# One 512-column product of the high weight part for both parts of a split activation

## The chip, the cores and the metric

The kernel runs on one core of a Trainium2 chip. The metric is the device time of one execution in microseconds, lower being better. Three runs of the kernel before gave 1787.77, 1788.87 and 1789.88 us. A core has a matrix engine (TensorE, PE in the profile; its weight loads are shown apart as PEld), a vector engine (DVE), a scalar engine (ACT), a general engine (POOL) and a queue engine (SP) that here issues most transfers from HBM.

## The reference

One layer on 256 tokens of width 2048: a normalised input, one large projection, four small branches (a gated recurrence, attention, a state-space branch, an RWKV branch), a gated merge, an output projection, a feed-forward part with a short convolution, and a per-layer embedding. Cut to its large products:

```python
xn = rmsnorm(h, mix_norm[i])
proj = jnp.einsum('bsd,dn->bsn', xn, w_in[i])
...
merged = merged + gates[:, :, j] * jnp.einsum('bsc,cd->bsd', branches[j], w_branch[i, j])
h = h + jnp.einsum('bsd,de->bse', merged, w_out[i])
hn = rmsnorm(h, ffn_norm[i])
u = causal_dwconv(jnp.einsum('bsd,df->bsf', hn, w_up[i]), ffn_conv_w[i], ffn_conv_b[i])
u_gate, u_val = jnp.split(u, 2, axis=-1)
h = h + jnp.einsum('bsf,fd->bsd', jax.nn.gelu(u_gate) * u_val, w_down[i])
pg = jax.nn.sigmoid(jnp.einsum('bsd,de->bse', rmsnorm(h, ple_norm[i]), w_ple_gate[i]))
h = h + pg * jnp.einsum('bsq,qd->bsd', p[i], w_ple[i])
```

All arrays are 32-bit floats.

## The kernel before

Every large product runs in a reduced 32-bit format (`fp32r`), with each operand written as a high part plus a low part. A weight w is wh + wl, an activation x is xh + xl, and the product is taken as wh·xh + wh·xl + wl·xh. Activations lie feature-major: 128 features on the partitions, 256 tokens along the free axis.

`gemm_fm` (L222) computes a unit of 256 output features, as two halves `m` of 128. It walks over the k blocks of 128 input features in chunks of four: one transfer of 128x1024 weights (`chunk`, L194, four buffers `wr`), then `split` (L199), which makes `wh` on ACT (L206) and `wl` on DVE (L207) in pieces of 128x512, six buffers each. For each m and each k, PE then does three products of 256 columns into the same PSUM tile: wh with xh, wh with xl, wl with xh. I call these three a triple. At the unit's end `evac` reads the PSUM tile, mostly with one DVE operation that also multiplies by the token's norm R.

The order of the stages: the projection `w_ax` (L43 of the start, with x loaded and split beside it by `load_x`), 19 units of the projection `w_p`, the 2-unit token-major `w_v` (`gemm_tm`, L265: its products stream 512 weight columns over stationary activations), then four rounds of gate units (`w_g`, 16 k blocks) and branch products (`w_branch`, 4 k blocks), then `w_out` (8 units), `w_up` (44 units), `w_down` (8 units of 44 k blocks), and `w_ple`/`w_ple_gate` (8 units). The small products of the four branches (`psB` banks, L135) are put between the large ones by `pump`, one step per m and chunk.

A scheduler orders the instructions of each engine from priorities: loads, splits and evacuations are in lane "g" and go first, the branches ("b") follow, the stream of products ("m") comes last except on PE. Each engine then runs its own list in order.

The names in the rows: `s`, `sb` and `f` are 128x256 activation tiles, `pg` and `pb` PSUM banks of 512 columns, `prm` and `prm2` parameter columns, L132 the stream's matmul and L135 the branches', L100 and L120 the DVE helpers `tt` and `stt`, L127 the ACT helper.

Of the kernel before, what the change touches and what calls it, by code (L numbers as in the profile page):

```python
# [14 lines left out]
P = 128  # L15
S = 256
# [11 lines left out]
# column offsets of the input projection  # L28
# [4 lines left out]
# rows of the parameter blocks that are turned into per-partition columns  # L33
# [52 lines left out]
def body(tc, T, out, dbg=None):  # L86
# [59 lines left out]
    # The stream of products goes first on every engine but the tensor engine,  # L146
    # where the branches' small products go first.
# [11 lines left out]
    sp = ctx.enter_context(tc.tile_pool(name="sp", bufs=57))  # L159
# [20 lines left out]
    def dslot():  # L180
        return dp.tile([P, 512], F32, name="d", tag="d")
# [9 lines left out]
    # --------------------------------------------------------------- products  # L191
# [19 lines left out]
    def split_act(src, scale=None, pool=sp):  # L211
        """hi/lo parts of an activation tile (scale: per-partition column or number)."""
        h, l = slot(F32R, pool), slot(F32R, pool)
        if scale is None:
            A.copy(h, src)
            tt(l, src, h.bitcast(F32), ALU.subtract)
        else:
            act(h, src, AF.Copy if isinstance(scale, float) else AF.Identity, scale=scale)
            stt(l, src, scale, h.bitcast(F32), ALU.mult, ALU.subtract)
        return h, l  # L220

    def gemm_fm(W, xs, evac, each=None):  # L222
# [4 lines left out]
        pts = [(gbank if m < 2 else bank)()[:, :S] for m in range(nm)]  # L227
        step = 1024 // ncol
        k0 = 0
        if each is not None:  # L230
            lane("m")
            for i in range(5):
                mm(pts[0], warm[:, :P], warm, start=i == 0, stop=False)
        while k0 < nk:
# [11 lines left out]
            for m in range(nm):  # L246
                ms = slice(m * P, m * P + P)
                for k in range(kn):
                    xh, xl = xs[k0 + k]
                    wh, wl = w[k]  # L250
                    first, last = k0 + k == 0 and not (each and m == 0), k0 + k == nk - 1
                    mm(pts[m], wh[:, ms], xh, start=first, stop=False)
                    mm(pts[m], wh[:, ms], xl, start=False, stop=False)
                    mm(pts[m], wl[:, ms], xh, start=False, stop=last)
# [10 lines left out]
    def gemm_tm(W, xs, evac):  # L265
        """out[token, 512 columns] = x W, x feature-major; W: [chunk, p, k * n]."""
        nk = len(xs)
        pts = [gbank() for _ in range(2)]
        for k0 in range(0, nk, 2):
# [3 lines left out]
            for t in range(2):  # L273
                tsl = slice(t * P, t * P + P)
                for k in range(2):
                    xh, xl = xs[k0 + k]
# [12 lines left out]
    def mm2(o, l, src, start=True, stop=True, pool=sp):  # L289
        """l^T src for an l that float32r holds exactly"""  # L290
# [993 lines left out]
```

## Time and profile before

| | |
|---|---|
| median of three runs | 1788.87 us |
| span of the profiled execution, first to last instruction | 1792.8 us |
| PE busy / weight loads busy | 1784.0 us / 1763.7 us |
| DVE busy / ACT busy | 1236.4 us / 987.8 us |
| matmul records | 14953 |
| HBM read | 324.85 MB |

The profiled execution is a run of its own; its span stands 3.9 us (0.2%) above the median of the runs. Busy shares of PE overlap (a matmul's record is longer than the step from one start to the next), so what PE needs per product is read from the starts in the timeline, not from the mean duration.

### The profile page before, as it was taken

To read this page: it belongs to the slowest core of one execution; us is meant where nothing else is said; L and a number is where in the kernel's file an instruction comes from. 1 tells how busy PE (TensorE), PEld (TensorE's weight loads), DVE (VectorE), ACT (ScalarE), POOL (GpSimd) and SP (SyncE) were. 2 spreads that over 40 slices of the span, in tenths; PEclk is the share of its full clock that TensorE was granted. 3 is DMA by queue.
4 is the path that set the end of the run, shared out by engine and by line. 5 is a ranking of instruction groups with operands and counts; after the bars stand their busy time and mean duration, and the time that the engine had idled before them with its cause. 6 is when DMAs were issued, how large, how long until landed. Compare 5 with 4: busy or idle time off the path is not lost.

```text
span 1792.8 us, 37987 instructions
## 1 busy us (share of the span) xinstructions
PE 1784.0 (100%) x14953; PEld 1763.7 (98%) x14953; DVE 1236.4 (69%) x2382; ACT 987.8 (55%) x1809; POOL 102.1 (6%) x160
## 2 busy tenths in 40 slices
PE   9999999999999999999999999999999999999998
PEld 8999899999999999999999999999999999999998
DVE  8778677687789533758677777777777755555665
ACT  7677455567744433645556555555555544444543
POOL 3000000012310100000110000000000100000000
PEclk9999999999999989999999999999999999999999
DMA  8566556567775733566766666565666766665564
GB/s 277 171 182 187 172 174 218 169 190 200 210 198 171 238 117 114 178 199 189 242 212 183 182 188 182 183 185 180 184 183 186 219 194 183 189 185 180 176 211 130
DMA packets 98883, 336.80 MB, mean 188 GB/s; under 512 B 12330, under 2 KB 16592, under 8 KB 98704
## 3 DMA queue, kind: packets, MB, share of 16 engines
q1 hardware_dynamic: 90528, 310.94, 57.0%
q0 software_dynamic: 7456, 21.81, 4.0%
q8 instruction: 117, 1.92, 0.4%
q10 hardware_dynamic: 720, 1.63, 0.2%
q14 instruction: 62, 0.51, 0.1%
HBM read 324.85 MB, written 9.48 MB: 186 GB/s over the span
## 4 chain that ended last, share of the span: by engine, by line
PE 97%; DMA 1%; DVE 1%; ACT 0%; issue 0%; POOL 0%; DVEq 0%
PE pg L132 92%; PE pb L135 5%; PE pb L132 1%; DMA wr<-in_w_ax_dram 1%; DMA e<-ssd_ac 0%; DVE wl L207 0%; ACT wh L206 0%; DVE s L120 0%; DMA ssd_ac<-sb 0%; ACT s L127 0%; DVE e L116 0%; DVE s L100 0%; POOL d L432 0%; DVE sb L114 0%; DVE sb L100 0%
## 5 line engine op out<-in xcount | busy, mean ns | idle before, releaser
L132 PE MATMUL pg<-s,wh 128*128 128x256 f32 (+1 forms) x6944 | 1269.8, 284 | 2.7 <-ACT s L127 1.9
L132 PEld LDWEIGHTS pg<-s,wh 128*128 128x128 f32 (+1 forms) x6944 | 1086.1, 192 | 7.0 <-ACT s L127 2.1
L207 DVE TENSOR_TENSOR wl<-wr,wh 128x512 fp32r<-128x512 f32 x1170 | 798.2, 690 | 401.4 <-ACT wh L206 326.5
L206 ACT CAST wh<-wr 128x512 fp32r<-128x512 f32 x1170 | 712.3, 618 | 575.9 <-PE pg L132 416.8
L132 PE MATMUL pg<-s,wl 128*128 128x256 f32 (+1 forms) x3472 | 985.0, 284 | 0.4 <-DVE wl L207 0.4
L132 PEld LDWEIGHTS pg<-s,wl 128*128 128x128 f32 (+1 forms) x3472 | 664.6, 192 | 2.7 <-issue 1.0
L132 PE MATMUL pg<-f,wh 128*128 128x256 f32 x1408 | 253.5, 283 | 0.0
L132 PEld LDWEIGHTS pg<-f,wh 128*128 128x128 f32 x1408 | 219.6, 192 | 0.0
L132 PE MATMUL pg<-f,wl 128*128 128x256 f32 x704 | 199.2, 283 | 0.0
L132 PE MATMUL pg<-sb,wh 128*128 128x256 f32 x768 | 141.0, 283 | 0.0
L132 PEld LDWEIGHTS pg<-f,wl 128*128 128x128 f32 x704 | 135.2, 192 | 0.0
L120 DVE SCALAR_TENSOR_TENSOR s<-s,prm 128x255 f32<-128x255 f32 (+1 forms) x208 | 99.7, 480 | 37.5 <-ACT s L127 37.5
L132 PEld LDWEIGHTS pg<-sb,wh 128*128 128x128 f32 x768 | 119.4, 190 | 0.4
L127 ACT ACTIVATE s<-s,prm 128x256 f32<-128x256 f32 (+1 forms) x120 | 69.0, 575 | 80.4 <-DVE s L100 80.4
L132 PE MATMUL pg<-sb,wl 128*128 128x256 f32 x384 | 108.3, 283 | 0.0
L127 ACT ACTIVATE s<-s 128x256 f32<-128x256 f32 x140 | 57.7, 414 | 59.2 <-DVE s L100 39.8
L100 DVE TENSOR_TENSOR s<-pg,R 128x256 f32<-128x256 f32 x152 | 63.6, 421 | 31.8 <-PE pg L132 30.9
L132 PEld LDWEIGHTS pg<-sb,wl 128*128 128x128 f32 x384 | 72.7, 190 | 0.3 <-issue 0.2
L127 ACT ACT_TABLE_LOAD x42 | 53.9, 1283 | 2.2 <-PEq L1274 1.2
L100 DVE TENSOR_TENSOR s<-s 128x256 f32<-128x256 f32 x126 | 52.5, 419 | 0.4
L100 DVE TENSOR_TENSOR sb<-sb 128x256 fp32r<-128x256 f32 (+4 forms) x78 | 32.0, 418 | 8.6 <-ACT sb L127 6.8
L127 ACT ACTIVATE sb<-sb 128x256 f32<-128x256 f32 (+4 forms) x69 | 27.8, 414 | 9.3 <-DVE sb L100 8.1
(208 smaller groups left out, 842.6 us busy)
## 6 DMA issues: line engine op xcount, KB each, us to landing
wr<-in_w_up_dram SPq DMA_DIRECT2D x176, 512.0 KB, 3.7
wr<-in_w_g_dram SPq DMA_DIRECT2D x128, 512.0 KB, 4.0
wr<-in_w_down_dram SPq DMA_DIRECT2D x88, 512.0 KB, 3.8
wr<-in_w_p_dram SPq DMA_DIRECT2D x76, 512.0 KB, 3.9
wr<-in_w_branch_dram SPq DMA_DIRECT2D x32, 512.0 KB, 4.3
wr<-in_w_out_dram SPq DMA_DIRECT2D x32, 512.0 KB, 4.2
wr<-in_w_ple_gate_dram SPq DMA_DIRECT2D x32, 512.0 KB, 4.3
wr<-in_w_v_dram SPq DMA_DIRECT2D x8, 512.0 KB, 4.3
```

The lines of the kernel that those rows point to most:

```text
L100: V.tensor_tensor(o, a, b, op=op)
L120: V.scalar_tensor_tensor(o, a, s, b, op0=op0, op1=op1)
L127: A.activation(o, i, f, **kw)
L132: return f(*a, **kw)
L135: f(*a, **kw)
L206: A.copy(wh, wr[:, k:k + n])
L207: V.tensor_tensor(wl, wr[:, k:k + n], wh.bitcast(F32), op=ALU.subtract)
```

## The change

The two parts of an activation now lie side by side in one tile x of 512 columns. A new function `product` replaces the triple by two matmuls: wh with all 512 columns, into both halves of the 512-column bank, and wl with the first 256 columns, into the first half. From the second k block on, wl goes before wh. The two halves of the bank are added when the unit is evacuated: `joined` copies the second half out on ACT and adds the first half on DVE. Gates, branch products, the small logits and `w_v` keep three products of 256 (or 512) columns, on slices of the same tiles (`halves`). `split` makes one ACT and one DVE instruction for a whole chunk of up to 1024 columns, with three buffers each in place of six of 512.

```diff
     def split(wr, kn, cols):
-        res, step = [], max(1, 512 // cols)
-        for k in range(0, kn, step):
-            n = min(step, kn - k)
-            wh = wp.tile([P, n, cols], F32R, name="wh", tag="wh", bufs=6)
-            wl = wp.tile([P, n, cols], F32R, name="wl", tag="wl", bufs=6)
-            A.copy(wh, wr[:, k:k + n])
-            V.tensor_tensor(wl, wr[:, k:k + n], wh.bitcast(F32), op=ALU.subtract)
-            res += [(wh[:, i], wl[:, i]) for i in range(n)]
-        return res
+        wh = wp.tile([P, kn, cols], F32R, name="wh", tag="wh", bufs=3)
+        wl = wp.tile([P, kn, cols], F32R, name="wl", tag="wl", bufs=3)
+        A.copy(wh, wr)
+        V.tensor_tensor(wl, wr, wh.bitcast(F32), op=ALU.subtract)
+        return [(wh[:, i], wl[:, i]) for i in range(kn)]
...
+    def split_x(src, scale=None, to=None):
+        t = xslot() if to is None else to
+        split_to(t[:, :S], t[:, S:], src, scale)
+        return t
...
+    def product(pt, xs, k, nk, ms, w, fresh=True):
+        wh, wl = w
+        x = xs[k]
+        if k == 0:
+            mm(pt, wh[:, ms], x, start=fresh, stop=False)
+            mm(pt[:, :S], wl[:, ms], x[:, :S], start=False, stop=False)
+        else:
+            mm(pt[:, :S], wl[:, ms], x[:, :S], start=False, stop=False)
+            mm(pt, wh[:, ms], x, start=False, stop=k == nk - 1)
...
+    def joined(o, pt):
+        A.copy(o, pt[:, S:])
+        add(o, o, pt[:, :S])
...
             lane("m")
-            for i in range(5):
+            for i in range(3):
                 mm(pts[0], warm[:, :P], warm, start=i == 0, stop=False)
...
+                    if not isinstance(xs[k0 + k], tuple):
+                        product(pts[m], xs, k0 + k, nk, ms, w[k], not (each and m == 0))
+                        continue
...
-    warm = slot()
+    warm = bc_.tile([P, 512], F32, name="e", tag="e", bufs=3)
...
             s = bslot()
-            tt(s, pt, R, ALU.mult)
+            joined(s, pt)
+            mul(s, s, R)
...
+    xg = [halves(x) for x in xs]
...
-        gemm_fm(T["w_g"][8 * j + u], xs, ev_g)
+        gemm_fm(T["w_g"][8 * j + u], xg, ev_g)
...
             h = slot()
-            add(h, pt, r)
-            xs_out.append(split_act(h, norm(k)))
+            joined(h, pt)
+            add(h, h, r)
+            xs_out.append(split_x(h, norm(k)))
...
             a, o = slot(), slot()
-            tt(a, pt, R2, ALU.mult)
+            joined(a, pt)
+            mul(a, a, R2)
...
-            o = slot()
-            mul(o, pt, R3)
+            o, e = slot(), slot()
+            joined(o, pt)
+            mul(o, o, R3)
             act(o, o, AF.Sigmoid)
-            mul(o, o, pe_[m])
+            joined(e, pe_[m])
+            mul(o, o, e)
```

On PE, in the middle of `w_up`, the list of before goes through the k blocks of one half m like this:

```order
L132 MATMUL pg<-s,wh 128x256 x2
L132 MATMUL pg<-s,wl 128x256
L132 MATMUL pg<-s,wh 128x256 x2
L132 MATMUL pg<-s,wl 128x256
L132 MATMUL pg<-s,wh 128x256 x2
L132 MATMUL pg<-s,wl 128x256
```

The list of now at the same place, four k blocks of one half m (the numbers are tile instances; `x` is the joint activation tile):

```order
L132 MATMUL pg_12178<-x_9792,wl_12205 128x256
L132 MATMUL pg_12178<-x_9792,wh_12204 128x512
L132 MATMUL pg_12178<-x_9802,wl_12205 128x256
L132 MATMUL pg_12178<-x_9802,wh_12204 128x512
L132 MATMUL pg_12178<-x_9906,wl_12205 128x256
L132 MATMUL pg_12178<-x_9906,wh_12204 128x512
L132 MATMUL pg_12178<-x_9916,wl_12205 128x256
L132 MATMUL pg_12178<-x_9916,wh_12204 128x512
```

Three matmuls per k block became two, and the 512-column one writes both halves of the bank. Over the whole list the matmuls go from 14524 to 11194.

On DVE, in `w_up`, the end of a gate unit before (`wl` splits with the evacuation of the two halves, `s` from `pg`, between them):

```order
L207 TENSOR_TENSOR wl_14459<-wr_14452,wh_14458 128x512
L100 TENSOR_TENSOR s_14402<-pg_14264,R_96 128x256
L120 SCALAR_TENSOR_TENSOR s_14403<-s_14402,prm2_81,s_14403 128x255
L100 TENSOR_TENSOR s_14409<-pg_14265,R_96 128x256
L207 TENSOR_TENSOR wl_14489<-wr_14486,wh_14488 128x512
L120 SCALAR_TENSOR_TENSOR s_14403<-s_14402,prm2_81,s_14403 128x254
L207 TENSOR_TENSOR wl_14493<-wr_14486,wh_14492 128x512
L120 SCALAR_TENSOR_TENSOR s_14410<-s_14409,prm2_81,s_14410 128x255
L207 TENSOR_TENSOR wl_14523<-wr_14520,wh_14522 128x512
```

And now, where the addition of the bank's first half stands ahead of the product with R:

```order
L209 TENSOR_TENSOR wl_12091<-wr_12088,wh_12090 128x1024
L100 TENSOR_TENSOR f_11953<-s_11945,f_11953 128x256
L100 TENSOR_TENSOR s_12046<-s_12046,pg_11956 128x256
L100 TENSOR_TENSOR s_12046<-s_12046,R_99 128x256
L209 TENSOR_TENSOR wl_12113<-wr_12110,wh_12112 128x1024
L120 SCALAR_TENSOR_TENSOR s_12047<-s_12046,prm2_84,s_12047 128x255
L100 TENSOR_TENSOR s_12055<-s_12055,pg_11957 128x256
L120 SCALAR_TENSOR_TENSOR s_12047<-s_12046,prm2_84,s_12047 128x254
L100 TENSOR_TENSOR s_12055<-s_12055,R_99 128x256
L209 TENSOR_TENSOR wl_12135<-wr_12132,wh_12134 128x1024
```

Between two splits there stand up to four short operations now, against up to three before, and each split is twice as long a piece.

On DVE at the very end of the kernel, after the last split of weights, before (`s` is the output tile, `pb` the product with `w_ple`, the third operand `s` of the last two the residual):

```order
L100 TENSOR_TENSOR s_23799<-pg_23661,R_96 128x256
L100 TENSOR_TENSOR s_23799<-s_23799,pb_23647 128x256
L100 TENSOR_TENSOR s_23805<-pg_23662,R_96 128x256
L100 TENSOR_TENSOR s_23799<-s_23799,s_22419 128x256
L100 TENSOR_TENSOR s_23805<-s_23805,pb_23648 128x256
L100 TENSOR_TENSOR s_23805<-s_23805,s_22427 128x256
```

And now:

```order
L100 TENSOR_TENSOR s_18441<-s_18441,pg_18351 128x256
L100 TENSOR_TENSOR s_18442<-s_18442,pb_18341 128x256
L100 TENSOR_TENSOR s_18441<-s_18441,R_99 128x256
L100 TENSOR_TENSOR s_18452<-s_18452,pg_18352 128x256
L100 TENSOR_TENSOR s_18453<-s_18453,pb_18342 128x256
L100 TENSOR_TENSOR s_18452<-s_18452,R_99 128x256
L100 TENSOR_TENSOR s_18441<-s_18441,s_18442 128x256
L100 TENSOR_TENSOR s_18441<-s_18441,s_17405 128x256
L100 TENSOR_TENSOR s_18452<-s_18452,s_18453 128x256
L100 TENSOR_TENSOR s_18452<-s_18452,s_17414 128x256
```

Six operations became ten, and after the last half's bank (`pg_18352`) is read there are six more on the list where there were three.

## Rows read from the trace of the kernel before

**Rows 1.** The head of the page: span, busy time of each engine (share of the span, instructions), the granted TensorE clock in 40 slices of the span, and the shares of the chain that ended last.

```profile
span 1792.8 us, 37987 instructions
PE 1784.0 (100%) x14953; PEld 1763.7 (98%) x14953; DVE 1236.4 (69%) x2382; ACT 987.8 (55%) x1809; POOL 102.1 (6%) x160
...
PEclk9999999999999989999999999999999999999999
...
PE 97%; DMA 1%; DVE 1%; ACT 0%; issue 0%; POOL 0%; DVEq 0%
```

**Rows 2.** Busy time in stretches of the span (us from its start; busy us and instruction count of PE, PEld, DVE, ACT, POOL; granted clock, DMA share, GB/s): gates beside the RWKV branch, `w_up`, `w_down`.

```profile
500.00:600.00 100.00, 100.00 (x839) 99.93 (x837) 93.51 (x174) 48.84 (x86) 9.99 (x16) 1.00 0.67 201
...
1000.00:1100.00 100.00, 100.00 (x836) 100.00 (x835) 72.27 (x140) 57.31 (x105) 0.00 (x0) 1.00 0.60 182
...
1600.00:1700.00 100.00, 100.00 (x836) 100.00 (x835) 58.07 (x95) 49.68 (x86) 0.00 (x0) 1.00 0.59 178
```

**Rows 3.** The same view of a stretch of gate products beside small branch products, with the stretch after it.

```profile
616.70:637.20 20.50, 20.50 (x161) 18.93 (x159) 4.46 (x8) 5.08 (x10) 0.00 (x0) 0.58 0.19 57
637.20:720.00 82.80, 82.80 (x945) 78.25 (x945) 33.16 (x61) 31.73 (x65) 1.51 (x2) 1.00 0.40 124
```

**Rows 4.** Who waited for whom over the whole span: us in total, times, longest.

```profile
ACT wh L206 <- PE pg L132: 416.8, 310, 4.4
DVE wl L207 <- ACT wh L206: 326.5, 299, 5.4
...
DVE wl L207 <- PE pg L132: 62.8, 44, 5.8
```

**Rows 5.** Timeline of PE in `w_up`: start, us, instruction, count. Products of 256 columns.

```profile
1000.09 0.28 PE L132 MATMUL pg<-s,wl 128*128 128x256 f32 x1
1000.21 0.40 PE L132 MATMUL pg<-s,wh 128*128 128x256 f32 x2
1000.45 0.28 PE L132 MATMUL pg<-s,wl 128*128 128x256 f32 x1
```

**Rows 6.** Timeline of PE in `w_v`, where the products have 512 columns. Between the first and the last of these rows lie twelve starts.

```profile
203.62 0.62 PE L132 MATMUL pg<-wh,s 128*128 128x512 f32 x2
204.08 0.39 PE L132 MATMUL pg<-wl,s 128*128 128x512 f32 x1
204.31 0.61 PE L132 MATMUL pg<-wh,s 128*128 128x512 f32 x2
...
206.35 0.61 PE L132 MATMUL pg<-wh,s 128*128 128x512 f32 x2
```

**Rows 7.** The transfers by tensor: count, KB each, median us to landing. Each of 512 KB is a chunk of four k blocks, that is eight triples.

```profile
wr<-in_w_up_dram SPq DMA_DIRECT2D x176, 512.0 KB, 3.7
...
wr<-in_w_down_dram SPq DMA_DIRECT2D x88, 512.0 KB, 3.8
wr<-in_w_p_dram SPq DMA_DIRECT2D x76, 512.0 KB, 3.9
...
wr<-in_w_out_dram SPq DMA_DIRECT2D x32, 512.0 KB, 4.2
wr<-in_w_ple_gate_dram SPq DMA_DIRECT2D x32, 512.0 KB, 4.3
```

**Rows 8.** Groups of DVE and of ACT instructions, shapes apart: count, busy us, mean ns of one, idle before.

```profile
L207 DVE TENSOR_TENSOR wl<-wr,wh 128x512 fp32r<-128x512 f32 x1170 | 798.2, 690 | 401.4 <-ACT wh L206 326.5 <-PE pg L132 62.8 <-ACT sb L913 1.9
L100 DVE TENSOR_TENSOR s<-pg,R 128x256 f32<-128x256 f32 x152 | 63.6, 421 | 31.8 <-PE pg L132 30.9
L100 DVE TENSOR_TENSOR s<-s 128x256 f32<-128x256 f32 x122 | 50.9, 419 | 0.4
L120 DVE SCALAR_TENSOR_TENSOR s<-s,prm 128x255 f32<-128x255 f32 x88 | 42.4, 481 | 28.8 <-ACT s L127 28.8
```

```profile
L206 ACT CAST wh<-wr 128x512 fp32r<-128x512 f32 x1170 | 712.3, 618 | 575.9 <-PE pg L132 416.8 <-issue 66.3 <-ACT s L127 29.7
L1169 ACT CAST f<-s 128x256 fp32r<-128x256 f32 x44 | 17.7, 401 | 0.0
L913 ACT COPY sb<-pb 128x256 f32<-128x256 f32 x14 | 5.2, 373 | 14.0 <-PE pb L135 14.0
```

**Rows 9.** Timeline of PE at the start: the warm-up products, the first real ones, and the two longest idle times after them.

```profile
1.23 4.63 PE L132 MATMUL pg<-s 128*128 128x256 f32 x10 [1.23 <-DVE s L330]
5.31 0.79 PE L132 MATMUL pg<-s,wh 128*128 128x256 f32 x2
...
13.53 0.51 PE L132 MATMUL pg<-s,wh 128*128 128x256 f32 x2 [1.93 <-ACT s L127]
...
14.83 0.39 PE L132 MATMUL pg<-s,wh 128*128 128x256 f32 x1 [0.56 <-DVE s L120]
```

**Rows 10.** Timeline of PE, DVE and ACT at the end of the span.

```profile
1788.01 0.28 PE L132 MATMUL pg<-s,wl 128*128 128x256 f32 x1
1788.33 0.42 DVE L100 TENSOR_TENSOR s<-pg,R 128x256 f32<-128x256 f32 x1
...
1788.79 0.42 ACT L127 ACTIVATE s<-s 128x256 f32<-128x256 f32 x1 [1.02 <-DVE s L100]
...
1789.69 0.43 DVE L100 TENSOR_TENSOR s<-s 128x256 f32<-128x256 f32 x1
```

More of the change, by code (lines that the diff above doesn't have):

```diff
@@ L178, in bslot, with dslot, xslot @@
         return slot(dt, bp)
-    def dslot():
-        return dp.tile([P, 512], F32, name="d", tag="d")
+    def dslot(dt=F32):
+        return dp.tile([P, 512], dt, name="d", tag="d")
+    def xslot():
+        return xp.tile([P, 512], F32R, name="x", tag="x")
     mixc = cst.tile([P, KD], F32, name="mixc")
@@ L219, in split_act, with halves @@
             stt(l, src, scale, h.bitcast(F32), ALU.mult, ALU.subtract)
+    def split_act(src, scale=None, pool=sp):
+        h, l = slot(F32R, pool), slot(F32R, pool)
+        split_to(h, l, src, scale)
         return h, l
+    def split_x(src, scale=None, to=None):
+        t = xslot() if to is None else to
+        split_to(t[:, :S], t[:, S:], src, scale)
+        return t
+    def halves(x):
+        return (x[:, :S], x[:, S:]) if not isinstance(x, tuple) else x
+    def product(pt, xs, k, nk, ms, w, fresh=True):
[10 more added lines that the diff above has]
+        add(o, o, pt[:, :S])
     def gemm_fm(W, xs, evac, each=None):
@@ L226, in gemm_fm @@
         nm, nk = ncol // P, KD if each else len(xs)
-        pts = [(gbank if m < 2 else bank)()[:, :S] for m in range(nm)]
+        pts = [(gbank if m < 2 else bank)() for m in range(nm)]
         step = 1024 // ncol
@@ L248, in gemm_fm @@
                 for k in range(kn):
+                    if not isinstance(xs[k0 + k], tuple):
+                        product(pts[m], xs, k0 + k, nk, ms, w[k], not (each and m == 0))
+                        continue
                     xh, xl = xs[k0 + k]
                     wh, wl = w[k]
[L251 to L254, printed above, removed]
+                    first, last = k0 + k == 0, k0 + k == nk - 1
+                    pt = pts[m][:, :S]
+                    mm(pt, wh[:, ms], xh, start=first, stop=False)
+                    mm(pt, wh[:, ms], xl, start=False, stop=False)
+                    mm(pt, wl[:, ms], xh, start=False, stop=last)
                 if hook[0]:
@@ L275, in gemm_tm @@
                 for k in range(2):
-                    xh, xl = xs[k0 + k]
+                    xh, xl = halves(xs[k0 + k])
                     wh, wl = w[k]
@@ L983, in small_logits @@
         for k in range(KD):
-            xh, xl = xs[k]
+            xh, xl = halves(xs[k])
             wh, wl = wt[k]
@@ L1082, in ev_z @@
             if last:
-                ms[k] = split_act(s, 0.5, bp if k < 8 else sp)
+                if k < 8:
+                    to = dslot(F32R)
+                else:
+                    if k % 4 == 0:
+                        mse.append(bc_.tile([P, 4, 512], F32R, name="e", tag="e", bufs=3))
+                    to = mse[-1][:, k % 4]
+                ms[k] = split_x(s, 0.5, to)
         gemm_fm(T["w_branch"][8 * j + u], ys[j], ev_z)
@@ L1167, in ev_val @@
             mul(o, o, gts[m])
-            hh, ll = fp.tile([P, S], F32R, name="f", tag="f"), fp.tile([P, S], F32R, name="f", tag="f")
-            A.copy(hh, o)
-            sub(ll, o, hh.bitcast(F32))
-            acts.append((hh, ll))
+            acts.append(split_x(o, None, fp.tile([P, 512], F32R, name="f", tag="f")))
         gemm_fm(T["w_up"][u], hs, ev_gate)
@@ L1179, in body @@
         nc.gpsimd.dma_start(s, T["pT"][k * P:k * P + P])
-        pTs.append(split_act(s))
+        pTs.append(split_x(s, None, pp_.tile([P, 512], F32R, name="p", tag="p")))
     acc2, h2s = [None], []
@@ L1199, in body @@
         lane("m")
-        pe_ = [bank()[:, :S] for _ in range(2)]
+        pe_ = [bank() for _ in range(2)]
         for m in range(2):
-            msl = slice(m * P, m * P + P)
             for k in range(2):
-                xh, xl = pTs[k]
-                wh, wl = w[k]
-                mm(pe_[m], wh[:, msl], xh, start=k == 0, stop=False)
-                mm(pe_[m], wh[:, msl], xl, start=False, stop=False)
-                mm(pe_[m], wl[:, msl], xh, start=False, stop=k == 1)
+                product(pe_[m], pTs, k, 2, slice(m * P, m * P + P), w[k])
         def ev_o(m, pt):
-            o = slot()
-            mul(o, pt, R3)
+            o, e = slot(), slot()
+            joined(o, pt)
+            mul(o, o, R3)
             act(o, o, AF.Sigmoid)
-            mul(o, o, pe_[m])
+            joined(e, pe_[m])
+            mul(o, o, e)
             add(o, o, h2[2 * u + m])
```

20 lines of the change are left out of this document (9 added, 11 removed).

## Prediction

> **What bounds the kernel now.** I read the head of the page first [rows 1]: PE is busy over the whole span and the chain that ended last is 97% PE, so the question is what one product costs PE. A busy share near 100% does not say that PE runs without gaps, because records overlap; the stage windows do [rows 2]. In `w_up` and in `w_down` PE starts 836 products of 256 columns in 100 us, one every 119.6 ns, and the two stages agree although DVE is busy 72% in one and 58% in the other. So nothing but the product itself sets the step there. The waits say the same from the other side [rows 4]: ACT stands 416.8 us waiting for PE to give a `wh` buffer back. The weight parts are ready ahead of PE, not late. ACT and DVE have room except in one stretch of the gates, where DVE is at 93.5% and PE still makes 839 starts [rows 2].
>
> The timeline shows the step [rows 5]: three products every 0.36 us. At the upper clock level, 2.4 GHz (granted clock 1.00 in these stretches), 256 columns stream in 106.7 ns, so about 13 ns of each step is not streaming. Is that a share of the columns, or a price per product? `w_v` answers, the one stage with 512 columns [rows 6]: from 203.62 to 206.35 us there are twelve starts, 227.5 ns each (226.7 over the nine from 204.31). 512 columns stream in 213.3 ns, which leaves 13 to 14 ns again. The extra is per product and does not grow with the columns.
>
> **The change part by part.**
>
> *PE, the term that decides.* A triple costs 3 x 119.6 = 358.8 ns. It becomes one product of 512 and one of 256 columns: 227.5 + 119.6 = 347.1 ns by these rows, or 2 x 13.3 + 320.0 = 346.6 with the extra taken as 13.3 throughout, against 360.0 for the triple. The saving is 11.7 to 13.4 ns; I take 12.5. The transfers give the count [rows 7]: 176 + 88 + 76 + 32 + 32 = 404 chunks of eight triples are 3232; `w_ple` adds 8 units x 2 halves x 2 k blocks = 32, together 3264. (`w_ax` has 16 x 4 = 64 more; the start has its own limit, below.) 3264 x 12.5 ns = 40.8 us. The trace of before has no alternation of 512 and 256 columns, so its price has bounds: at best the columns alone, 320.0 ns, 3264 x 38.8 = 127 us saved; at worst no less than today, 0 saved. I take the value of the two rows because each of them is a dense stream of just this instruction.
>
> All of this rests on the extra being paid per weight load and not hidden. The Trainium skill says otherwise (TensorE: Matmul & The Clock Gate, on what happens when a matmul is issued and on the back-to-back issue gap): the next weights load while the current product streams, and the step is N / 2.4 GHz plus about 2.5 ns. By that rule a product less would save 2.5 ns, an estimate of 3264 x 2.5 = 8 us in all. The trace does not agree, with 13 ns beyond the streaming at both widths; the rule stays as part of a rival.
>
> *Splits.* 1170 pieces of 512 columns become 578 of 1024 and 14 of 512 on each engine. From 256 to 512 columns a DVE operation goes from 419 to 690 ns and an ACT cast from 401 to 618 [rows 8]; carried on, 1024 columns are 1.23 us on DVE and 1.05 on ACT (bounds from above: twice the 512 piece, 1.38 and 1.24). DVE gains 578 x 0.15 = 87 us of busy time, ACT 578 x 0.18 = 104 us. Both lie beside PE and give nothing by themselves.
>
> *Evacuation.* 194 banks now need a copy on ACT (0.37 us, the nearest row is the copy out of a PSUM tile) and one DVE operation more (0.42) [rows 8]: ACT +72 us, DVE +81. On balance each engine's load hardly moves. Behind a copy that waits for PE's last product of a half stand the next casts on ACT's list, and behind these DVE's splits and PE. But the next cast in line needs the buffer of the chunk that holds that same last product, so it could not start earlier anyway. I cost it at nothing.
>
> *Cover for PE.* A buffer of 1024 columns is given back when PE has finished the chunk, and is wanted again two chunks later: 2 x 8 x 347 ns = 5.55 us. The cast and the split take 1.05 + 1.23, which leaves 3.27 us. Between two splits DVE's list has at most four short operations, 2 x 0.42 + 2 x 0.48 = 1.8 us [rows 8]. That fits, so no stall is counted. If that cover fails, the cost is one stall at each of the 87 changed units (19 + 8 + 44 + 8 + 8). SP's transfers wait for the split's end as they do now, and in the last stage the outputs that stand between them on SP's queue come about a microsecond later; the two chunks already split cover that too.
>
> *Start.* The warm-up is 3 products of 512 columns in place of 5 of 256: each record took (5.31 - 1.23) / 10 = 0.41 us [rows 9], so 4.9 us in place of 4.1. Later PE idles 1.93 and 0.56 us for x [rows 9], which swallows the 0.8 us. Larger first splits may delay a chunk; I count +0.5 us, with bounds of -0.8 (the 64 triples' gain arrives whole) and +3.
>
> *End.* From the last matmul's end, 1788.29, to the last DVE end, 1790.12, lie 1.8 us [rows 10]. By the new list the last half needs a copy and seven DVE operations in a row (the other half's two fill the time of the sigmoid): 0.37 + 7 x 0.42 = 3.3 us, +1.5 us.
>
> *Clock.* From 616.7 to 637.2 us the granted clock averages 0.58, the lower level for most of it, after dense runs of 64-row branch products between gate products [rows 3]. Gates keep their three products and the branch products keep their places in PE's list, so I expect the same dip. About 17 of these 20.5 us are at 1.2 GHz; without the dip up to 8.6 us would go, with a second one as much would come.
>
> Sum, against the profiled execution: 1792.8 - 40.8 + 0.5 + 1.5 = 1754.0 us of span. The median of the runs lies 3.9 us below the span, so 1750 us.
>
> **Rivals.**
>
> *The extra is not saved (5%).* It might belong to the alternation of wh and wl, or return in the mixed order. For it: no row has 512 and 256 in turn. Against it: both widths show the same 13 ns. The span would be 1792.8 + 2.0, the time 1791. With the step that the Trainium skill states (the same page) it would be 1783, an estimate.
>
> *The short product's load hides under the long one (5%).* Weight loads are busy 98% of the span [rows 1], so a stream of 256 columns might be too short to cover a load and one of 512 long enough. Then the 256-column product costs its columns alone, 227.5 + 106.7 = 334.2 ns, 24.6 saved, 80 us: 1711. Against it: a product of 512 columns should then show no extra today, and it shows 13 [rows 6].
>
> *Coarse pieces starve PE, slower (5%).* One `wl` of 1024 columns is ready only as a whole, and PE now wants `wl` ahead of `wh` in all but the first k block. If evacuations and the longer pieces queue so that each of the 87 units costs PE a stall of t, the time is 1750 + 87 t: no gain from t = 0.45 us, slower by over 0.2% from 0.49, and 1802 us at 0.6. For it: DVE waited 62.8 us for PE and 326.5 for ACT [rows 4], so its order is not free of waits, and at 93.5% in the gates [rows 2] it has little left. Against it: the 3.27 us above, DVE's splits get cheaper in just that stretch, and ACT waits for PE far longer than the reverse. A small t, up to 0.2 us, would cost 17 us and is inside my range.
>
> **How the numbers follow.** The forecast case has 85%, with its own spread: 11.7 to 13.4 ns per triple is 1747 to 1753, the clock adds 8.6 either way, small stalls up to 17 us above. The rivals have 5% each. The range is 1740 to 1767. What a measurement of this kernel can tell from no change is about 0.2%, 3.6 us. Faster by more than that: the forecast, the hidden load and a part of the unsaved extra, 92%; within: 4%; slower: 4%.
>
> **What would show it.** In `w_up` and `w_down` the starts should come in pairs, 0.347 us per k block and half, so about 576 in 100 us; `wl` splits should read about 1.23 us and `wh` casts 1.05. PE should show no idle time at the units' ends, the copies about 0.37 us each. The last DVE operation should end some 3.3 us after the last matmul, and the dip of the clock should stand after the same branch products. The forecast is wrong if the pair takes 0.36 us or 0.335, or if steps of several hundred ns appear at a chunk's first `wl`.

## The result and the profile after

The changed kernel takes 1779.54 us (median of ten runs, 1771.53 to 1786.13), the kernel before 1788.39 us beside it (ten runs, 1786.04 to 1794.86): a ratio of 0.994, 95% interval 0.9919 to 0.996. It is faster by more than the 0.2% that can be told apart, as forecast, but by 9 us and not by 38: the time lies 12.5 us above the upper end of the range.

The mean granted clock is not the same in each execution of one program, and the time goes with it: the ten runs of the changed kernel go from 1786.13 us at a clock of 0.989 to 1771.53 us at 0.997. At 0.996 to 0.997 it takes 1771.5 to 1774.8 us, and the kernel before at the same clock 1789.8 to 1792.6 us (in its runs beside the experiments). At an equal clock the change is worth about 17 us.

The head of the page of after, with the lines that answer to [rows 1]:

```profile
span 1781.4 us, 29735 instructions
...
PE 1761.6 (99%) x11621; PEld 1586.7 (89%) x11621; DVE 1239.1 (70%) x1998; ACT 942.8 (53%) x1422; POOL 103.2 (6%) x160
...
PEclk9999999999999979999999999999999999999999
...
PE 72%; issue 8%; DMA 1%; DVE 1%; POOL 0%; ACT 0%; POOLq 0%; DVEq 0%
```

The matmuls went from 14953 to 11621 records, DVE and ACT hardly moved, and PE still bounds the kernel; in the chain, though, it has 72% where it had 97%. Stretches of the span of after (columns as in [rows 2]): a piece of the RWKV branch's small products beside gates, `w_up`, `w_down`.

```profile
621.00:648.40 27.40, 27.40 (x190) 24.59 (x189) 6.17 (x9) 6.53 (x11) 0.00 (x0) 0.56 0.18 58
1000.00:1100.00 100.00, 100.00 (x568) 86.88 (x567) 76.58 (x126) 56.91 (x89) 0.00 (x0) 1.00 0.59 188
1500.00:1600.00 100.00, 100.00 (x576) 87.45 (x575) 52.59 (x61) 44.07 (x54) 1.07 (x2) 1.00 0.62 191
```

I call the 512-column and the 256-column product of one k block and half a pair. `w_down` makes 576 starts in 100 us, the number of the forecast (0.347 us per pair). `w_up` makes 568, which is 0.352 us per pair. The next two views are the groups of instructions (count, busy us, mean ns of one, idle before) and the waits (us in total, times, longest) of after, against [rows 8] and [rows 4]:

```profile
L209 DVE TENSOR_TENSOR wl<-wr,wh 128x1024 fp32r<-128x1024 f32 (+1 forms) x592 | 717.3, 1213 | 433.1 <-ACT wh L208 425.3
L208 ACT CAST wh<-wr 128x1024 fp32r<-128x1024 f32 (+1 forms) x592 | 615.4, 1040 | 664.1 <-PE pg L132 519.7
L132 PE MATMUL pg<-x,wl 128*128 128x256 f32 (+1 forms) x3344 | 923.5, 284 | 10.1 <-DVE wl L209 10.1
...
L249 ACT COPY s<-pg 128x256 f32<-128x256 f32 x136 | 49.6, 366 | 46.7 <-PE pg L132 46.2
```

```profile
PE pg L132 <- DVE wl L209: 10.1, 7, 3.8
PE pg L132 <- DVE sb L100: 2.4, 2, 1.4
```

The pieces cost what was forecast (1.21, 1.04, 0.37 us). New is the idle time of PE: seven waits for `wl` (before, one of 0.4 us), and two for a bank that the evacuation's add had not yet read.

By stages, from the first `wl` product of each in the two timelines (us, before and after): up to the last branch products 810.3 and 818.9; from there to `w_out` 22.5 and 22.5; `w_out` 91.09 and 89.87; `w_up` 507.12 and 496.98; `w_down` 253.44 and 245.89; the last stage 108.3 and 107.2. The second half of the kernel gained 20 us, the first lost 8.6.

The longest stall, in the timelines of PE, DVE and ACT of after (start, us, instruction, count, idle before it):

```profile
163.39 0.40 PE L132 MATMUL pg<-x,wh 128*128 128x512 f32 x1
167.62 0.58 PE L132 MATMUL pg<-x,wl 128*128 128x256 f32 x1 [3.83 <-DVE wl L209]
168.00 0.63 PE L132 MATMUL pg<-x,wh 128*128 128x512 f32 x1
...
170.55 0.39 PE L132 MATMUL pg<-x,wh 128*128 128x512 f32 x1
...
171.25 0.40 PE L132 MATMUL pg<-x,wh 128*128 128x512 f32 x1
```

```profile
159.42 1.22 DVE L209 TENSOR_TENSOR wl<-wr,wh 128x1024 fp32r<-128x1024 f32 x1 [2.19 <-ACT wh L208]
161.90 0.42 DVE L100 TENSOR_TENSOR sb<-sb,pg 128x256 f32<-128x256 f32 x1 [1.25 <-ACT sb L249]
162.34 1.66 DVE L116 TENSOR_SCALAR e<-e,ssd_col 128x128 f32<-128x128 f32 x8
163.91 0.87 DVE L114 TENSOR_SCALAR sb<-sb,prm 128x256 f32<-128x256 f32 x3
164.70 0.42 DVE L100 TENSOR_TENSOR sb<-sb,R 128x256 f32<-128x256 f32 x1
165.03 0.42 DVE L100 TENSOR_TENSOR sb<-sb,pg 128x256 f32<-128x256 f32 x1
165.37 1.07 DVE L116 TENSOR_SCALAR e<-e,ssd_col 128x128 f32<-128x128 f32 x5
166.34 1.22 DVE L209 TENSOR_TENSOR wl<-wr,wh 128x1024 fp32r<-128x1024 f32 x1
```

```profile
157.81 0.63 ACT L127 ACTIVATE d<-d 128x512 f32<-128x512 f32 x1 [4.70 <-DMA d<-ssd_ac]
158.35 1.03 ACT L208 CAST wh<-wr 128x1024 fp32r<-128x1024 f32 x1
159.40 1.28 ACT L127 ACT_TABLE_LOAD   x1
160.70 0.91 ACT L127 ACTIVATE sb<-sb,prm 128x256 f32<-128x256 f32 x2
161.51 0.35 ACT L249 COPY sb<-pg 128x256 f32<-128x256 f32 x1
```

Read from below: ACT stands 4.7 us for a load of the state-space branch, so its next cast comes late, and the copy of an evacuation, with a table load of 1.28 us and two branch operations between them, later still. DVE stands 2.19 us for the cast, then 1.25 us for the copy, and has sixteen branch operations and three evacuation steps in its list ahead of the next `wl`. PE runs dry after the product of 163.39. The first pairs behind the stall are slow too: four of them take 2.55 us from 168.00 on (0.64 each), the two from 170.55 on 0.70 (0.35 each). The granted clock was at its lower level, 1.2 GHz, from 167.1 to 170.5.

The end of the span of after, against [rows 10]: the last matmul ends at 1775.62, the last DVE operation 3.1 us later (forecast 3.3).

```profile
1777.06 1.68 DVE L100 TENSOR_TENSOR s<-s 128x256 f32<-128x256 f32 x4
```

### The profile page after: what moved, and what is told of

The parts are those of the page before. It is cut to its first block, busy times and chain, and to the rows that moved or that the text cites. A ratio compares the mean times of both kernels' runs of the same rounds, so it can differ in the third digit from the quotient of the medians.

```text
span 1781.4 us, 29735 instructions
## 1 busy us (share of the span) xinstructions
PE 1761.6 (99%) x11621; PEld 1586.7 (89%) x11621; DVE 1239.1 (70%) x1998; ACT 942.8 (53%) x1422; POOL 103.2 (6%) x160
## 4 chain that ended last, share of the span: by engine, by line
PE 72%; issue 8%; DMA 1%; DVE 1%; POOL 0%; ACT 0%; POOLq 0%; DVEq 0%
PE pg L132 70%; PE pb L135 1%; PE pb L132 1%; DMA e<-fox_rn 0%; DVE wl L209 0%; DMA d<-rw_gn 0%; DMA rw_q<-e 0%; DMA rw_gn<-sb 0%; DVE s L100 0%; DVE e L888 0%; DVE sb L120 0%; POOL qbd L903 0%; POOL e L927 0%; DVE e L100 0%; POOL qat L899 0%
## 5 line engine op out<-in xcount | busy, mean ns | idle before, releaser
L132 PE MATMUL pg<-x,wh 128*128 128x512 f32 (+1 forms) x4384 | 1194.6, 346 | 2.4 <-DVE sb L100 2.4
L209 DVE TENSOR_TENSOR wl<-wr,wh 128x1024 fp32r<-128x1024 f32 (+1 forms) x592 | 717.3, 1213 | 433.1 <-ACT wh L208 425.3
L208 ACT CAST wh<-wr 128x1024 fp32r<-128x1024 f32 (+1 forms) x592 | 615.4, 1040 | 664.1 <-PE pg L132 519.7
L132 PE MATMUL pg<-x,wl 128*128 128x256 f32 (+1 forms) x3344 | 923.5, 284 | 10.1 <-DVE wl L209 10.1
L132 PEld LDWEIGHTS pg<-x,wh 128*128 128x128 f32 x4384 | 757.1, 190 | 100.8 <-issue 2.6
L132 PEld LDWEIGHTS pg<-x,wl 128*128 128x128 f32 (+1 forms) x3344 | 635.0, 190 | 24.9 <-DVE wl L209 12.9
L132 PE MATMUL pg<-f,wh 128*128 128x512 f32 x704 | 244.9, 395 | 0.0
L132 PEld LDWEIGHTS pg<-f,wh 128*128 128x128 f32 x704 | 131.6, 188 | 29.8
L100 DVE TENSOR_TENSOR s<-s 128x256 f32<-128x256 f32 (+1 forms) x172 | 70.7, 420 | 1.4
L100 DVE TENSOR_TENSOR s<-s,pg 128x256 f32<-128x256 f32 x136 | 56.3, 415 | 10.0 <-ACT s L249 8.3
```

The costliest lines, as they stand in the source:

```text
L100: V.tensor_tensor(o, a, b, op=op)
L132: return f(*a, **kw)
L208: A.copy(wh, wr)
L209: V.tensor_tensor(wl, wr, wh.bitcast(F32), op=ALU.subtract)
```

## The experiments

Two things were open: what made the stalls, and why a pair costs 0.352 us in `w_up` and 0.347 in `w_down`. Theory A of the stalls is the 1024-column pieces, theory B the joined evacuation.

**Splits of 512 columns in the changed kernel.**

```diff
-        wh = wp.tile([P, kn, cols], F32R, name="wh", tag="wh", bufs=3)
-        A.copy(wh, wr)
+        for k in range(0, kn, step):
+            wh = wp.tile([P, n, cols], F32R, name="wh", tag="wh", bufs=6)
+            A.copy(wh, wr[:, k:k + n])
...
```

> The change with its splits put back to pieces of 512 columns, six buffers each; products, joined evacuations and all else stay as changed. Theory A (the pieces of 1024 columns stall PE while the branches run: DVE's list holds a long split behind a branch step that waits, and the clock falls after the stall): the stalls of 4.2 us at 163 us and 2.2 us at 758 us go, the branch products' last round starts near 805 instead of 819 us of the span, and the time falls by 8 to 16 us, to about 1768. Theory B (the joined evacuation and the denser branch steps make these stalls, the size of the pieces does not matter): same stalls, 1780 give or take 4 us. Both: w_up stays at 353 ns per k block and half.

1765.69 us (1765.36 to 1770.84), ratio 0.9865 [0.9841, 0.9888]. After 28 us of the span PE takes no step over 0.5 us, and the last branch products begin at 798.6 us instead of 818.9. (Not all of these 20 us are the stalls': the RWKV stretch had 3.4 us at the lower clock here and 23.9 in the profile of the changed kernel.) Theory B, by which the size of the pieces doesn't matter, fails. The same place on DVE in this kernel:

```profile
163.05 0.69 DVE L212 TENSOR_TENSOR wl<-wr,wh 128x512 fp32r<-128x512 f32 x1 [1.16 <-ACT wh L211]
163.66 0.67 DVE L116 TENSOR_SCALAR e<-e,ssd_col 128x128 f32<-128x128 f32 x3
164.24 0.48 DVE L120 SCALAR_TENSOR_TENSOR sb<-sb,prm 128x255 f32<-128x255 f32 x1
164.64 0.48 DVE L116 TENSOR_SCALAR e<-e,ssd_col 128x128 f32<-128x128 f32 x2
165.03 0.48 DVE L120 SCALAR_TENSOR_TENSOR sb<-sb,prm 128x255 f32<-128x255 f32 x1
165.43 0.28 DVE L116 TENSOR_SCALAR e<-e,ssd_col 128x128 f32<-128x128 f32 x1
165.62 0.69 DVE L212 TENSOR_TENSOR wl<-wr,wh 128x512 fp32r<-128x512 f32 x1
```

Eight small operations lie between these two splits, where there were nineteen; the wait for a cast is 1.16 us, and the next piece comes in time. `w_up` is unchanged (497.12 us): the price of the pair has nothing to do with the stalls.

**Splits of 1024 columns alone, in the kernel before.**

```diff
-        for k in range(0, kn, step):
-            wh = wp.tile([P, n, cols], F32R, name="wh", tag="wh", bufs=6)
+        wh = wp.tile([P, kn, cols], F32R, name="wh", tag="wh", bufs=3)
...
```

> The kernel before with only its splits made in pieces of up to 1024 columns, three buffers each; its three products of 256 columns stay. Theory A: new stalls while the branches run, 6 to 14 us slower than before, about 1797. Theory B: no new stall, within 3 us of before, 1788. Both: w_up stays at 360 ns per triple.

1792.22 us, ratio 1.0015 [0.9997, 1.0034]. DVE is busy 1171.6 us instead of 1236.4 and ACT 886.2 instead of 987.8, and the time doesn't move; PE has one new step over 0.8 us after the start (1.56, at 45.5 us). So theory A fails too as it stands: the coarse pieces alone stall nothing much.

**The changed kernel with `w_ax` and `w_p` back at three products and one evacuation step, pieces of 1024 kept.**

```diff
-            joined(s, pt)
-            mul(s, s, R)
+            tt(s, pt[:, :S], R, ALU.mult)
...
-    gemm_fm(T["w_ax"], xs, evac_raw(raw["ax"]), load_x)
+    xh_ = Halved(xs)
+    gemm_fm(T["w_ax"], xh_, evac_raw(raw["ax"]), load_x)
...
-            gemm_fm(T["w_p"][u0 + u], xs, evac_raw(raw[name]))
+            gemm_fm(T["w_p"][u0 + u], xh_, evac_raw(raw[name]))
```

> The change without its part in w_ax and w_p: these projections do three products of 256 columns on slices of the joint tile and evacuate with one DVE operation; splits of 1024 columns and everything from w_out on stay as changed. Theory A (pieces of 1024 columns): the stalls stay and the 8 us that the projections save are gone, 1782 to 1790. Theory B (joined evacuation and denser steps): the stalls go, the last round of branch products starts near 811 us as before, about 1771.

> The changed kernel with w_ax and w_p alone put back to three products on halves and a single-operation evacuation, 1024-column splits kept (the earlier run of it was timed at 1769.8 us, but its profile was taken at a clock of 0.45). Wanted is the profile. Theory that the stalls of the branch phase need both the 1024-column pieces and the joined evacuation: no stall of PE over 2.6 us after the start, and the start of the last branch stage at 800 to 808 us, against 818.9 us as changed. Theory that the coarse pieces alone do it: a stall of 3 us or more near 163 us and one near 757 us again, and the last branch stage at 815 us or later.

1769.77 us in the timed runs (1768.55 to 1773.76), ratio 0.9884 [0.986, 0.9907]: the kernel that gives up the change in 672 of its pairs is 10 us below the changed one's median of ten runs, and 5 us below that of its repeat (further down). The second run, a single one, took 1779.04 us; its profile has one stall, 2.65 us at 22.8, and after it no step over 0.81 us.

The last branch products begin at 814.9 us in it, outside the 800 to 808 that was expected, because 20.5 us between 620.8 and 644.7 went at the lower clock, in the RWKV stretch where the kernel before has its own dip [rows 3]. On the stalls: pieces of 1024 with three products and single-step evacuations have none over 1.6 us behind the first 28 us, pieces of 512 with joint products and joined evacuations have none over 0.5, and both changes together have 1.8 at 121, 4.2 at 163 and 2.2 at 757 us. (The stall between 21 and 28 us is another matter: it stands here, in the changed kernel and with 512-column pieces alike, 2.65, 3.04 and 2.47 us.) A and B are each half right. This run undid the joint product together with the joined evacuation, so which of these two it takes beside the coarse pieces is not shown; no run changed one of them without the other.

**Which link of it? The evacuation's copy on DVE instead of ACT, and the changed kernel once more beside it.**

```diff
-        A.copy(o, pt[:, S:])
+        V.tensor_copy(o, pt[:, S:])
```

> The changed kernel with one line turned: the copy of the bank's second half in the joined evacuation goes to VectorE in place of ScalarE, so that VectorE's list waits for ScalarE no more at an evacuation. Theory F (VectorE, held at an evacuation's add by ScalarE's copy that stands behind a cast, a table load or a wait for a load, brings the next wl late; that is what the coarse pieces and the joined evacuation do together): the stalls at 163 us (4.2) and 757 us (2.2) go, the last branch stage starts before 810 us, the median falls to 1766 to 1774 us. Theory G (the 1024-column pieces simply stand behind too many branch operations in VectorE's list): VectorE has 136 x 0.4 us more to do, the stalls stay or grow, 1778 to 1788 us.

> The changed kernel once more, on the same chip and in the same rounds as the one with the copy on VectorE. Wanted is how far its time and its stalls hold from chip to chip. If the stalls of the branch phase are in its program (waits of a list in order), the profile has PE stalls of over 2 us near 163 and 757 us again and the last branch stage at 812 to 822 us, and the median is 1772 to 1786 us. If they were the accident of one execution, the last branch stage starts near 802 us and the median is 1764 to 1770 us.

With the copy on DVE 1782.04 us (1775.38 to 1789.26), ratio 0.9958 [0.9937, 0.9979]. The time is the one that theory G had, but neither theory held whole. The stalls near 163 and 757 us shrink, as theory F had it, to 1.66 us (at 173.2) and 0.73 us (at 766.5); a worse one came up at another place of the list, where PE waits for a bank to be read:

```profile
129.63 0.77 PE L132 MATMUL pg<-x,wh 128*128 128x512 f32 x1 [5.55 <-DVE sb L100]
```

```profile
PE pg L132 <- DVE wl L209: 8.8, 8, 2.7
PE pg L132 <- DVE sb L100: 6.6, 2, 5.5
```

At that place DVE stood 1.55 us for a cast and 1.67 us for a step of the recurrence on ACT before it came to the evacuation, and by then PE wanted the bank. Moving one step moves the stall, it doesn't end it.

The changed kernel again: 1774.72 us (1771.05 to 1778.85), ratio 0.9916 [0.9888, 0.9944]. Its profile repeats the stalls at 22.4 (3.02), 123.1 (1.80) and 165.9 us (4.15): they belong to the program. The one at 757 us does not repeat (0.64), and the last branch products begin at 810.7 us, just below the 812 to 822 that was expected. Two stretches of this profile, the one at the stall and the RWKV stretch:

```profile
165.90:176.00 10.10, 6.34 (x21) 5.15 (x20) 9.67 (x26) 6.25 (x13) 0.00 (x0) 0.66 0.33 107
620.00:648.00 28.00, 28.00 (x315) 25.64 (x314) 8.57 (x11) 9.12 (x16) 0.00 (x0) 1.00 0.35 111
```

After the stall the clock falls again, 6.8 us this time. But the RWKV stretch, at clock 0.56 in the first profile, is at 1.00 here, 315 starts in 28 us: the same program had that dip in one execution and not in the other. Between the same two groups of branch products around it pass 56.5 us (from 605.66 on) and 46.5 us (from 610.49 on).

**The price of a pair: four long products, then four short ones.** Theory C is that alternating them costs extra, theory D that a product of 512 columns costs that much beside anything.

```diff
+                    for ph in ("l", "h") if tail else ("h", "l"):
+                        for k in range(kn):
...
```

> The change with the products of one chunk and half grouped: four of 512 columns (wh), then four of 256 (wl), in the last chunk the other way round. Theory C (the taking in turn of 512 and 256 columns falls into a pattern of three k blocks, 113 + 233 + 117 + 241 + 120 + 236 ns, that costs 353 ns a k block; dense runs of one width do not): w_up falls to 347 ns or less per k block and half, 9 us there and 4 elsewhere, about 1766. Rival D (each product of 512 columns costs more for this operand, whatever the order): w_up stays at 353, time 1776 to 1783.

1769.87 us (1766.47 to 1771.58), ratio 0.9881 [0.9858, 0.9904]. The time is nearer to C, but `w_up`, on which the two differ, takes 494.21 us, 11.23 per unit where the changed order takes 11.29: 351 ns a pair, nearer to D. Its stalls stand at other places, the longest 2.48 us at 119.3; with another order of the products the scheduler writes other lists.

**Seven orders in one run, by units of `w_up`.**

```diff
-        gemm_fm(T["w_up"][u], hs, ev_gate)
+        gemm_fm(T["w_up"][u], hs, ev_gate, var=VARS[2 * u])
...
```

> The changed kernel with 512-column splits; the 44 units of w_up go through seven arrangements of the products of one weight chunk, in a shuffled order, so that one profile holds about six units of each: 0 lo, hi per k block as the change has it; 1 four hi then four lo; 2 hi lo lo hi (pairs turned about); 3 the two halves of the columns taken in turn (hi hi lo lo); 4 as 0, but the lo product goes into the second half of the bank; 5 three products of 256 columns into the halves of the bank; 6 as 0, but the lo weights stream both activation tiles too (512 columns; this adds the product lo times lo, which the reference's splitting leaves out). A unit as changed takes 11.29 us in w_up (353 ns per k block and half). Theory C (alternating long and short products costs extra, 6 to 7 ns a pair): orders 1 and 2 go to 11.10 to 11.15 us per unit, 0, 3 and 4 stay at 11.29. Theory D (a product of 512 columns costs some 233 ns in w_up whatever stands beside it): 0 to 4 all 11.2 to 11.3, and order 6, which is nothing but long products, 32 x 2 x 233 = 14.9 us. Theory E (the two patterns are phases of one stream that a unit's start sets, and the order that a unit had before decides): units of order 0 come out at both 11.1 and 11.3 in one run. The control 5 should take 11.5 us (32 x 359 ns); if it takes less, the bank, and not the joining, makes part of the gain.

One unit to a row, from its first start to the next unit's (columns as in [rows 2]; orders 2, 3, 6, 5, 4, 1 as the expectation numbers them, then a unit of order 0):

```profile
919.22:930.37 11.15, 11.15 (x65) 9.74 (x64) 8.59 (x19) 8.97 (x17) 0.00 (x0) 1.00 0.55 182
930.37:941.52 11.15, 11.15 (x65) 9.74 (x64) 10.71 (x24) 7.61 (x17) 0.00 (x0) 1.00 0.64 194
941.52:956.03 14.51, 14.51 (x66) 12.02 (x64) 8.92 (x18) 7.67 (x16) 0.00 (x0) 1.00 0.50 159
956.03:967.51 11.48, 11.48 (x94) 11.31 (x93) 9.59 (x20) 7.09 (x14) 0.00 (x0) 1.00 0.52 169
967.51:978.79 11.28, 11.28 (x66) 9.80 (x64) 8.63 (x17) 7.05 (x15) 0.00 (x0) 1.00 0.58 186
978.79:989.98 11.19, 11.19 (x65) 9.80 (x64) 9.53 (x21) 6.72 (x15) 0.00 (x0) 1.00 0.58 188
1038.00:1049.29 11.29, 11.29 (x65) 9.82 (x64) 8.55 (x16) 6.97 (x14) 0.00 (x0) 1.00 0.55 172
```

The kernel took 1780.47 us in its one run, with orders 5 and 6 in it; what counts are its units. Those of a kind agree within 0.03 us, but for the first unit (11.52, with two small products of another kind in it) and one of order 4 (11.12). Nothing but long products (order 6): 64 in 14.51 us, 227 ns each, so theory D falls; a long product beside long ones costs in `w_up` just what it costs in `w_v` [rows 6]. Three short ones (order 5, 92 products of which four are long): 11.48 us, 120 ns for a short one, so writing to both halves of the bank has no price of its own. The mixed orders cost, in the median of their units, 11.14 (turned about), 11.15 (both halves in turn), 11.20 (four and four) and 11.29 (as changed), where the two pure prices give 11.10; the second half of the bank as target of the short product (order 4) changes nothing. In single starts the changed order goes 113, 233, 117, 241, 120, 236 ns, the order by halves 113, 119, 233, 236, 116, 112, 233, 231.

So the order moves the price, as theory C has it, and in `w_up` units of order 0 come out alike whatever stood before them, against theory E. But C is not whole either. The expectation had order 3 stay at 11.29. Four and four, with half as many changes from long to short as orders 2 and 3, costs more than they do. And the changed order has two prices in `w_down`, as the first two units of the changed kernel (88 pairs each) show:

```profile
1427.86:1458.94 31.08, 31.08 (x178) 26.98 (x176) 18.40 (x26) 14.40 (x19) 2.15 (x4) 1.00 0.66 204
1458.94:1489.47 30.53, 30.53 (x177) 26.91 (x176) 16.16 (x19) 13.65 (x17) 0.54 (x1) 1.00 0.63 194
```

That is 353 and 347 ns a pair. The first, fourth and seventh of the eight units take the one, the others the other, so something like the phases of theory E is at work there. What it is in the order that costs is not shown.

**That order in every joint product, with 512- and with 1024-column splits.**

```diff
+            for k in range(kn if joint else 0):
+                x, (wh, wl) = xs[k0 + k], w[k]
+                last = k0 + k == nk - 1
+                for t in "lh" if last else "hl":
+                    for m in range(nm):
...
```

> The changed kernel with 512-column splits, and in every joint product the two halves of the columns in turn: hi hi lo lo per k block (lo lo hi hi in the last) in place of lo, hi, lo, hi. In the run that mixed the orders these units of w_up took 11.03 to 11.14 us against 11.28 to 11.39. Theory C (the order of long and short products sets the price of a pair, in all stages): w_up 486 us (from 497.1), w_down 243 (from 248.6), w_out, the projections and the last stage 4 to 5 us together, no new stall: 1765.7 - 21.5 = 1744 us, 1741 to 1750. Theory E (the stream has phases that a unit takes over from the one before; when all units have one order it may settle in a dearer phase, as four hi and four lo did: 11.23 alone, 11.09 among others): w_up 490 to 497 us, 1753 to 1766 us in all.

> The changed kernel with its 1024-column splits, with the order of the run before alone (hi hi lo lo). Theory C with the stalls due to the lists of VectorE and ScalarE, which this doesn't touch: the same price of a pair as with 512-column splits (w_up 486 us), the last branch stage at 808 to 818 us with a stall of 3 to 4 us near 165 us, and 1774.7 - 11.2 - 3 - 4 = 1756 us, 1750 to 1763. Rival: the lo product, now 0.23 us later behind its hi product, gives VectorE so much more room that the stalls go: the last branch stage before 802 us and the time within 3 us of the 512-column kernel. If the price of a pair hangs on the split's tiles too, w_up differs from the 512-column kernel by over 2 us.

With 512-column splits 1755.45 us (1753.32 to 1763.11), ratio 0.9813 [0.979, 0.9835]: the fastest of all, and within the range that was forecast for the change. `w_up` takes 491.56 us, 11.17 per unit, `w_down` 245.39. The 11.03 to 11.14 us from which the expectation starts were read from windows that lay two products off the units; by the rows above a unit goes from 11.29 to 11.15, which promises 6.2 us in `w_up`, and 5.6 came. So the order by halves costs the same alone as among others (11.17 and 11.15), and four and four does too (11.23 and 11.20). The 490 to 497 us of theory E contain the result, but in `w_up` no phase that a unit takes over is needed for it. The head and two stretches (the branch phase, `w_up`) of this profile:

```profile
span 1751.4 us, 31709 instructions
...
PEclk9999999999999999999999999999999999999999
```

```profile
150.00:180.00 30.00, 30.00 (x170) 25.81 (x169) 28.84 (x75) 23.42 (x46) 2.38 (x4) 1.00 0.66 217
...
1000.00:1100.00 100.00, 100.00 (x575) 87.33 (x574) 80.86 (x163) 64.37 (x126) 0.00 (x0) 1.00 0.57 189
```

PE isn't idle in the stretch where the changed kernel stalled longest, its last branch products begin at 795.0 us, and the clock stays at its upper level until the end. With 1024-column splits the same order takes 1772.09 us (1764.96 to 1777.11), ratio 0.9895 [0.9872, 0.9918]. `w_up` is the same to 0.04 us (491.52), so the gap of 17 us arises before it: a stall of 1.5 us is left at 163 us, where the changed kernel had 4.2, another of 1.7 at 249.6; in its profile 20.5 us of the RWKV stretch ran at the lower clock, an estimated 9 us of the gap, and the last branch products begin at 812.9 us. The stalls shrank more than the one theory had it and less than the rival, and the time lies above what either had.

```profile
150.00:180.00 30.00, 28.28 (x154) 24.00 (x153) 27.25 (x63) 19.99 (x32) 1.95 (x4) 0.94 0.66 213
600.00:660.00 60.00, 60.00 (x539) 56.20 (x539) 20.13 (x27) 17.83 (x25) 2.07 (x3) 0.83 0.48 149
```

## Why the prediction was wrong in size

The profiled execution took 1781.4 us where the sum said 1754.0, so 27.4 us are to be found.

- **"That fits, so no stall is counted."** This is the step that failed, and it cost most: the last branch products begin 8.6 us later than before, where the sum had them 7.1 us earlier (608 pairs at 12.5 ns, less 0.5 at the start), 15.7 us in all. The step set 3.27 us of cover against at most four short operations between two splits. I had read that number in the list of `w_up`, where it holds, and carried it to the branch phase, where sixteen branch operations and three evacuation steps stand between two splits. It also left out that DVE in that list waits for ACT, once for the cast and once for the evacuation's copy, while ACT itself stands 4.7 us for a load. Seven steps between 20 and 760 us lasted 0.6 to 4.2 us, 14.2 together; the longest of the kernel before in that stretch is 0.64. The 15.7 us are those of one execution: in the repeat's profile, which had the stalls but not the dip of the clock in the RWKV stretch, the last branch products begin 0.4 us later than before, 7.5 us behind the sum.
- **The evacuation: "I cost it at nothing", and the splits beside it.** Neither stalls PE for long by itself, as the runs show (1024-column splits alone 1.0015; joint products and joined evacuation with 512 columns have no stall after 28 us). I priced the edits one by one, and the loss is in them together: a longer piece that comes later, behind a list that waits for another engine twice.
- **"I expect the same dip" of the clock.** The lower level held for 31 us of the profiled execution, against 17 before. A pair takes 0.64 us at that level instead of 0.35, so the 14 us more cost an estimated 6 of the 15.7 us. About 7 us of them stand right behind the two stalls (167.1 to 170.5, 761.0 to 764.5); the rest is the RWKV stretch, which differs from one execution of a program to the next, and lies inside the 8.6 us that the prediction gave it.
- **"12.5 ns" per triple.** Right in `w_down` for most units (7.6 us gained of 8.8) and too large in `w_up`: a pair takes 353 ns there, 7 saved. 10.1 of 17.6 us came; over `w_out`, `w_up`, `w_down` and the last stage together 11.7 us less than the sum had. The step took the price of a mixed stream as the sum of two pure ones. The run with seven orders shows both pure prices to be right, 227 and 120 ns, and the mixture to cost from 348 to 353 by its order, never less than the 347 of the sum.
- **What was right.** The direction; the price of a short and a long product by themselves; the saving being per product; 1.23, 1.05 and 0.37 us for split, cast and copy; the end; no stall at a unit's end in `w_up`. The Trainium skill (TensorE: Matmul & The Clock Gate, Back-to-back issue gap) gives N / 2.4 GHz plus about 2.5 ns for the gap of a single product, and with that as the step the time would have been 1783 us, an estimate. The median lies nearer to that than to my 1750, but not for its reason: the pure steps in the run with seven orders are 227 and 120 ns, 13 to 14 ns above the streaming as in [rows 5, 6].
- **The rivals.** The coarse pieces that starve PE are what happened, but not at each of the 87 units: at seven places before 760 us. The prediction held a stall of 0.2 us per unit for possible, 17 us in all, and the stalls with the clock behind them took about that much; the pair price came on top of it.

Shown by runs: the long stalls behind the first 28 us need the coarse pieces and the joint products with their evacuation together, those at 121 and 163 us belong to the program, and the order moves the price of a pair. Not separated: the joint product and the joined evacuation. Argued only: that the clock's fall at 167 us follows from the stall; it followed the long stall in both profiles of the changed kernel and is missing at that place in the two with 512-column splits. Open: what in the order costs, what lets the same list of pairs run at 347 or at 353 ns (`w_down` in the changed order takes 245.89 us with 1024-column splits in each profile and 248.60 with 512), and when the RWKV stretch gets its dip.

## What to carry to other kernels

A cover that is worked out in one stage holds for that stage; count the operations between two producers in the list of each stage, and the waits for other engines that stand among them. Price two edits that lean on the same engine together, since what each can afford alone the pair may not. Where instructions of two lengths are to be mixed, the sum of their pure prices need not be met, and the order is worth a run of its own: here 11.14 to 11.29 us for the same products, where the sum is 11.10.

## What the runs showed of the hardware

- 64 products of 512 columns with 64 different weights run at 227 ns each (in `w_v` and in `w_up`) and 256-column ones at 120 (in `w_up`, `w_down` and the gates); alternated they take 353 ns per pair in `w_up` and 347 or 353 in `w_down`, two long then two short 348 to 349.
- At the upper clock level a product costs 13 to 14 ns beyond its columns. At the lower one no such extra shows: from 168.00 to 170.55 us of the changed kernel four pairs take 2.55 us, 0.64 each, which is their 768 columns at 1.2 GHz.
- A stall of PE of 2.2 to 6 us was followed by 3.4 to 6.8 us at the lower clock level in several profiles (in the changed kernel after those at 163.4 and 757.6), but one of 3.04 us at 21.9 in the same profile was not.
- The same program had 23.9 us at the lower level in the RWKV stretch in one execution and none in another, 10 us of its time.
